# A third pair of k-tiles in the last half-pass of w_down, and five more loads

## The chip, the cores and the metric

The kernel runs on one core of one Trainium2 chip. The metric is the device time of one execution in microseconds (us). A core has engines with queues of their own, each in program order: TensorE (PE, with its weight loads as PEld), VectorE (DVE), ScalarE (ACT), GpSimd (POOL) and SyncE (SP), which here only issues DMAs. POOL issues DMAs too, among them those that add to what stands at the destination (accumulating DMAs). The kernel's order on every queue is the order in which the program text emits instructions; nothing is rescheduled afterwards.

## The reference

One layer of a hybrid block on 256 tokens of width 2048, in float32:

```python
xn = rms_norm(h, norm1_g[l])
proj = jnp.einsum('bsd,dn->bsn', xn, w_in[l])          # 2048 x 5120
...
h = h + jnp.einsum('bsm,md->bsd', mixed, w_out[l])     # mixed: attention and convolution, 2048 x 2048
hn = rms_norm(h, norm2_g[l])
a = jnp.einsum('bsd,df->bsf', hn, w_gate[l])           # 2048 x 5632
bu = jnp.einsum('bsd,df->bsf', hn, w_up[l])
h = h + jnp.einsum('bsf,fd->bsd', jax.nn.silu(a) * bu, w_down[l])   # 5632 x 2048
```

The change touches the last product, with w_down, and three loads elsewhere.

## The kernel before

**Precision.** Each float32 operand is split into hi (rounded to the matmul type, by ScalarE) and lo, the residue (operand minus hi, by VectorE). A product is three matmuls: hi with hi, lo with hi, hi with lo. A weight tile's residue is made in one of two ways: VectorE subtracts (L334), or ScalarE writes the negated copy (L328) and a POOL DMA adds the weights to it (L329). The second way takes work from VectorE and gives ScalarE and POOL some; a unit for which it is used has `by_dma` set.

**Units.** Weights are worked off in units (`chunks`), each with its load (SP), cast (ACT), residue and matmuls. Two kinds matter here:
- a "two" (`load_chunk`, `round_chunk`, `split_chunk`, `multiply_two`): two k-tiles of 128 rows, 512 columns of weights, for both halves m of the tokens: 2 x 2 x 3 = 12 matmuls. In w_down a "g" two belongs to the first 512 of a block of 1024 columns and a "u" two to the second; for the same two k-tiles both are needed.
- a "pair" ("s": `load_pair`, `round_pair`, `split_pair`, `multiply_pair`): two k-tiles k and k + 4, both column halves, both token halves as a 2 x 2 block product in Strassen's form with seven products instead of eight: 7 x 3 = 21 matmuls instead of 24. For that VectorE makes four sums of weight blocks (L1019 to L1021), ScalarE casts (L1022 the blocks, L1025 the sums) and VectorE makes residues (L1028 `wlb` of the blocks, L1029 `wlt` of the sums). The first product of a pair uses a sum, so its third matmul waits for `wlt`.

**w_down in passes.** The hidden dimension is done in groups of 4, 4 and 3 blocks of 512 (`FGROUPS`). After each group `down_pass` multiplies the group's k-tiles with w_down: two half-passes, i = 0 and 1, one for each 1024 columns of the output (n = 2 i). `NDS` says how many pairs a group's pass has; k-tiles 0 to 3 and 4 to 7 of a group can be paired, the others are twos. `DORDERS` writes out the order of the units of each half-pass. The last group (nb = 3, 12 k-tiles) has two pairs and four g and four u twos per half-pass; its second half-pass runs in the order g g g s g s u u u u.

**Forms of the activations.** `transposed` turns a block of silu(a) * up into k-tiles through the PE, two k-tiles (t = 0, 1) at a time. For tiles that are paired it keeps the raw copy (`raw_act`), for others hi and lo. When the second block of a group is through, `make_down_forms` makes the seven sums of activations and their residues, 11 VectorE and 7 ScalarE operations over nd k-tiles each, spread over the next block.

**Order and looking ahead** (`run_chunks`). Before the matmuls of unit t are emitted, units up to t + 2 have been cast and split; if a pair stands among units t to t + 3, casting (for a pair also L1019 to L1021) reaches to t + 3. Loads are emitted when the unit whose buffer they take has been split, or, if that unit's residue comes by DMA, not before its own matmuls' turn; plain weights have five buffers, pairs two. Casts have three buffers, so a cast waits for the PE to finish with the unit three before.

**What ends a half-pass.** After its last pair or g unit, `bank_sums` adds the eight PSUM banks up (L1156 to L1163); `down_half` and `down_whole` add the results into h, which lies in HBM (`hd`), by accumulating POOL DMAs (L1210, L1238). In the very last half-pass they are added in SBUF instead: `fetch_end` (L1200) loads h's last 1024 columns as `hend` when the first half-pass ends, L1212, L1217, L1278 and L1231 add, and the rows are stored. The first 1024 columns of the output are copied from `hd` (L1245).

**Other loads of the change.** `late_loads` (L185) loads the rope table ahead of unit 9; `x_whole` (L1298) loads x in token-major form ahead of unit 40. Both on SP's queue.

Of the kernel before, what the change touches and what calls it, by code (L numbers as in the profile page):

```python
# [18 lines left out]
P = 128  # L19
D = 2048  # L20
S = 256
NM = S // P
# [9 lines left out]
N = 512  # L32
# [52 lines left out]
ORDER = "sggsggsuusuu"  # L85
# [1 line left out]


HD = N // P
NDS = (4, 4, 2)  # L90
DORDERS = {4: (ORDER, ORDER), 3: ("gguusggsuu", "gggsgsuuuu")}
HD_LAG = 3
DOWN_BY_DMA = {4: (dict(g=(0, 1), u=(1,)),) * 2, 3: (dict(g=(), u=()),) * 2}

Q1, Q6, Q7, Q5, Q2, Q4, Q3, QX = range(8)

# [31 lines left out]
def tile_block(  # L128
# [6 lines left out]
    act, dve, pool, pe, sp = nc.scalar, nc.vector, nc.gpsimd, nc.tensor, nc.sync  # L135
# [13 lines left out]
    h = [pre.tile([P, D], F32, tag=f"h{m}", name=f"h{m}", bufs=1) for m in range(NM)]  # L149
    away = ctx.enter_context(tc.tile_pool(name="away", bufs=1, space=bass.MemoryType.DRAM))  # L150
    hd = [away.tile([P, D], F32, tag=f"hd{m}", name=f"hd{m}") for m in range(NM)]
# [25 lines left out]
    rt = pre.tile([P, NM, 2, DH], F32, tag="vb", name="rt")  # L177
# [3 lines left out]
    def late_loads():  # L181
        sp.dma_start(out=cw.rearrange("p c w -> p (c w)"), in_=conv_w)
        for t, v in ((gb, vecs[:2]), (lamv, vecs[2:])):
            sp.dma_start(out=t, in_=v.rearrange("(o v) d -> o v d", o=1).to_broadcast(list(t.shape)))
        sp.dma_start(out=rt, in_=rope.rearrange("(m p) c d -> p m c d", p=P))  # L185

    def late_constants():
        late_loads()
# [43 lines left out]
    def lhs_two(pfx, k):  # L232
        return tuple(lhs.tile([P, 2, S], F32R, tag=f"l{x}", name=f"{pfx}{x}{k}") for x in ("hi", "lo"))
# [12 lines left out]
    def start(gen):  # L246
        running.append(gen)
# [7 lines left out]
    def lag(n):  # L255
        for _ in range(n):
            yield
# [593 lines left out]
    def up_done(j, ps):  # L851
        fp = ffn["pool"]
        aa = []
        for m in range(NM):
            a = fp.tile([P, N], F32, tag=f"sum{2 + m}", name="a")
            dve.scalar_tensor_tensor(a, ps[m], rstd2[m], sil[m], ALU.mult, ALU.mult)
            aa.append(a)
        yield from lag(4)
        yield from transposed(j, aa)

    def transposed(j, aa):
        last = j + 1 in FIRSTS and NDS[group_of(j)[0]] < HD
        b = j - group_of(j)[1]
        for t in range(N // P // 2):

            pool_, tag = (acc_ps, "acc") if last else (aux_ps, "aux")
            pt = pool_.tile([P, 2, S], F32, tag=tag, name="ps_a")
            for i in range(2):
                for m in range(NM):
                    c = (2 * t + i) * P  # L870
                    pe.transpose(pt[:, i, m * P : (m + 1) * P], aa[m][:, c : c + P], ident)  # L871
            g = group_of(j)[0]
            nd = NDS[g]
            if b < 2 and 2 * t < nd:
                if not b and not t:
                    raw_act[g] = ffn["pool"].tile([P, 2, nd, S], F32, tag="draw", name="raw_act")
                act.copy(raw_act[g][:, b, 2 * t : 2 * t + 2, :], pt)
                yield from lag(3 if last else 6)
                if b and 2 * t + 2 == nd:
                    start(make_down_forms(g))  # L880
                continue
            hi, lo = lhs_two("a", j * (N // P) + 2 * t)
            act.copy(hi, pt)
            yield from lag(1 if last else 2)
            dve.tensor_tensor(lo, pt, hi.bitcast(F32), ALU.subtract)
            for i in range(2):
                actT[j * (N // P) + 2 * t + i] = (hi[:, i, :], lo[:, i, :])
            yield from lag(1 if last else 3 if closing(j) else 4)

    def closing(j):  # L890
        return j + 1 in FIRSTS and NDS[group_of(j)[0]] == HD

    def group_of(j):

        j0 = 0
        for g, nb in enumerate(FGROUPS):
            if j < j0 + nb:
                return g, j0
            j0 += nb

    raw_act = {}
    down_forms = {}

    def make_down_forms(g):

        nd = NDS[g]
        gap = lambda: lag(5 if FGROUPS[g] == 4 else 2)
# [195 lines left out]
    def fast_block(order, pairs, twos, sources, operands, half, whole, by_dma=dict(g=(), u=())):  # L1103

        units, sums = [], {}
        left = dict(s=list(pairs), g=list(twos), u=list(twos))
        for kind in order:
            what = left[kind].pop(0)
            c = dict(kind=kind, sums=sums, done=None, first={}, last={}, rows=what["rows"], **operands)
            if kind == "s":  # L1110
                c.update(p=what["p"], fetch=load_pair, by_dma=False, round=round_pair, split=split_pair, multiply=multiply_pair,
                         uses=[q for q, _, _ in PRODUCTS])
                c["from"] = sources
            else:
                w, col = sources[kind]
                c.update(ks=what["ks"], w=w, nk=2, width=N, cols=[(col, N)], by_dma=what["k"] in by_dma[kind],
                         load=load_chunk, round=round_chunk, split=split_chunk, multiply=multiply_two,
                         uses=(Q3, QX) if kind == "u" else (Q2, Q4))
            units.append(c)
        assert not any(left.values())  # L1120
        for q in range(8):
            users = [c for c in units if q in c["uses"]]
            users[0]["first"][q] = users[-1]["last"][q] = True
        [c for c in units if c["kind"] != "u"][-1]["done"] = half
        units[-1].update(done=whole, prompt=True)
        chunks.extend(units)
# [8 lines left out]

    def down_pass(g, j0, nb):
        k0 = j0 * HD
        nd = NDS[g]
        ks = [k for k in range(nb * HD) if k >= 2 * HD or k % HD >= nd]
        twos = [dict(ks=(k0 + a, k0 + b), rows=slice(k0 + a, k0 + b + 1, b - a), k=i)  # L1140
                for i, (a, b) in enumerate(zip(ks[::2], ks[1::2]))]
        for i, order in enumerate(DORDERS[nb]):
            n = 2 * i
            end = {}
            fast_block(order, [dict(p=p, rows=slice(k0 + p, k0 + p + HD + 1, HD)) for p in range(nd)], twos,
                       dict(g=(w_down, n * N), u=(w_down, (n + 1) * N)),
                       dict(pairs=lambda: down_forms.get(g), plain=actT.get),
                       lambda sums, n=n, end=end: down_half(g, n, sums, end),
                       lambda sums, n=n, end=end: down_whole(g, n, sums, end), DOWN_BY_DMA[nb][i])

# [23 lines left out]
    def block_done(j, q):  # L1174
        while "u" not in halfway:
            yield
        u = halfway.pop("u")
        for m, i in enumerate((Q3, QX)):
            dve.tensor_tensor(u[m], q[i], u[m], ALU.add)
        while "g" not in halfway:  # L1180
            yield
        g = halfway.pop("g")
        for m in range(NM):
            dve.tensor_tensor(u[m], u[m], g[m], ALU.mult)
        yield from lag(6 if closing(j) else 4)
        yield from transposed(j, u)


    hend = []
# [4 lines left out]
    def fetch_end():  # L1194

        t = ffn["pool"].tile([P, 7, NS, P], F32, tag="fhi", name="hend")
        t = t.rearrange("p a b c -> p (a b c)")
        for m in range(NM):
            hend.append(t[:, m * 2 * N : (m + 1) * 2 * N])
            sp.dma_start(out=hend[m], in_=hd[m][:, D - 2 * N :])  # L1200

    def down_half(g, n, q, end):
        gs, us = yield from bank_sums(q)
        if not at_end(g, n):
            end.update(us=us)
            yield from lag(HD_LAG)
        for m in range(NM):
            cs = slice(n * N, (n + 1) * N)
            if not at_end(g, n):
                pool.dma_start(out=hd[m][:, cs], in_=gs[m], accum_op=ALU.add)  # L1210
            else:
                dve.tensor_tensor(hend[m][:, :N], hend[m][:, :N], gs[m], ALU.add)  # L1212
                pool.dma_start(out=out[m * P : (m + 1) * P, cs], in_=hend[m][:, :N])
        yield
        if at_end(g, n):
            for m in range(NM):
                dve.tensor_tensor(hend[m][:, N:], hend[m][:, N:], us[m], ALU.add)  # L1217
        end.update(us=us)
# [76 lines left out]

    def x_whole():
        for m in range(NM):
            sp.dma_start(out=h[m], in_=x[m * P : (m + 1) * P, :])  # L1298

    for i in range(OPENING):  # L1300
        before[i] = opening(i)
# [31 lines left out]
```

## Time and profile before

| | |
|---|---|
| runs shown | 1036.13 us median of 3 (1036.13 to 1036.54) |
| the profiled execution | 1035.99 us, of which span 1034.2 us |
| granted TensorE clock | 1.000 |
| last w_down pass, second half: first matmul | 998.36 us after the span's start |
| HBM read and written | 204.24 MB and 9.44 MB |

How to read the lines: a timeline row has start, duration, engine, source line, operation, output tile <- input tiles, shape, count, and in brackets the engine's idle time before it with what ended it. Matmuls are pipelined, so their shown durations (0.39 us) overlap; the distance between starts is what one costs. A group row ends in total busy time and mean ns, then idle time before it. "q" after an engine's name marks its queue issuing a DMA. "DMA to landing" is the time from issue until the data is there.

### The profile page before, as it was taken

The numbers are of one execution on the slowest core, as the hardware profiler recorded it, in microseconds if no ns is written. First come the engines' busy times: TensorE is split into PE (matmuls) and PEld (weight loads), VectorE is DVE, ScalarE is ACT, GpSimd is POOL, SyncE is SP. The second block draws the span as 40 slices with busy tenths as digits, with TensorE's granted clock in tenths as the row PEclk, the third lists the DMA queues.
The fourth block names the chain that finished last, engine by engine and source line by source line (L and its number), as shares of the span: only waits on it lengthen the run. The fifth ranks groups of instructions, "written<-read, shape, count | busy, mean of one in ns | idle before, by whom it ended". The sixth has DMA issues, their size and how long they took to land.

```text
span 1034.2 us, 13010 instructions
## 1 busy us (share of the span) xinstructions
PE 1028.1 (99%) x4645; PEld 848.9 (82%) x4645; DVE 927.3 (90%) x1126; ACT 638.3 (62%) x780; POOL 108.7 (11%) x147
## 2 busy tenths in 40 slices
PE   9999999999999999999999999999999999999998
PEld 7888888888888888888888888888888888888886
DVE  7899999989766699999999898989999989989887
ACT  7554656655666575677666556667657556667452
POOL 0130112111000100100102111001001111000010
PEclk9999999999999999999999999999999999999999
DMA  9657654553546677987989899879798979797773
GB/s 340 225 182 276 215 175 145 183 183 135 183 171 223 189 258 226 286 256 211 260 260 257 265 255 271 267 225 261 230 270 248 280 214 298 231 262 230 218 219 106
DMA packets 115664, 237.59 MB, mean 230 GB/s; under 512 B 7696, under 2 KB 8848, under 8 KB 115344
## 3 DMA queue, kind: packets, MB, share of 16 engines
q1 hardware_dynamic: 104720, 203.58, 59.0%
q0 software_dynamic: 10592, 33.04, 16.5%
q8 instruction: 36, 0.59, 0.2%
q14 instruction: 28, 0.23, 0.1%
q10 hardware_dynamic: 288, 0.16, 0.1%
HBM read 204.24 MB, written 9.44 MB: 207 GB/s over the span
## 4 chain that ended last, share of the span: by engine, by line
PE 96%; DVE 2%; DMA 1%; issue 1%; ACT 0%; SPq 0%; DVEq 0%
PE acc L364 11%; PE acc L365 11%; PE acc L370 11%; PE q L1067 11%; PE q L1068 11%; PE q L1073 11%; PE q L1048 9%; PE q L1046 9%; PE q L1047 9%; PE ps_a L871 1%; DVE wlo L334 1%; DMA raw<-in_w_in_dram 1%; PE ps_s L692 1%; PE ps_o L762 1%; DVE wlt L1029 0%
## 5 line engine op out<-in xcount | busy, mean ns | idle before, releaser
L325 ACT CAST whi<-raw 128x1024 fp32r<-128x1024 f32 (+1 forms) x257 | 266.4, 1047 | 149.7 <-PE acc L365 87.5
L334 DVE TENSOR_TENSOR wlo<-raw,whi 128x1024 fp32r<-128x1024 f32 (+1 forms) x211 | 254.6, 1217 | 37.9 <-ACT whi L325 37.8
L1025 ACT CAST wh<-wt 128x2048 fp32r<-128x2048 f32 x60 | 114.9, 1915 | 108.8 <-DVE wt L1021 108.7
L1029 DVE TENSOR_TENSOR wlt<-wt,wh 128x2048 fp32r<-128x2048 f32 x60 | 137.4, 2290 | 19.5 <-ACT wh L1025 19.4
L364 PE MATMUL acc<-whi,xhi 128*128 128x512 f32 x320 | 127.2, 398 | 0.7 <-ACT whi L325 0.6
L1067 PE MATMUL q<-whi,chi 128*128 128x512 f32 x320 | 125.2, 391 | 0.0
L365 PE MATMUL acc<-whi,xlo 128*128 128x512 f32 x320 | 125.1, 391 | 0.0
L1068 PE MATMUL q<-whi,clo 128*128 128x512 f32 x320 | 124.6, 389 | 0.0
L1046 PE MATMUL q<-wh,fhi 128*128 128x512 f32 x280 | 109.9, 392 | 0.0
L1047 PE MATMUL q<-wh,flo 128*128 128x512 f32 x280 | 108.9, 389 | 0.0
L1028 DVE TENSOR_TENSOR wlb<-wb,wh 128x1536 fp32r<-128x1536 f32 x60 | 105.1, 1751 | 1.1 <-ACT wh L1022 1.1
L553 DVE SCALAR_TENSOR_TENSOR y<-upad,cw,y 128x256 f32<-128x256 f32 x240 | 102.2, 485 | 2.2 <-ACT y L546 2.2
L329 POOL DMA_DIRECT2D wlo<-raw x46 | 39.8, 865 | 508.0 <-ACT wlo L328 283.4
L1022 ACT CAST wh<-wb 128x1536 fp32r<-128x1536 f32 x60 | 88.3, 1472 | 0.0
L370 PE MATMUL acc<-wlo,xhi 128*128 128x512 f32 x320 | 87.1, 393 | 0.0
L1073 PE MATMUL q<-wlo,chi 128*128 128x512 f32 x320 | 85.6, 389 | 0.0
L1067 PE MATMUL q<-whi,ahi 128*128 128x512 f32 x190 | 74.1, 390 | 0.0
L1068 PE MATMUL q<-whi,alo 128*128 128x512 f32 x190 | 74.0, 389 | 0.0
L1019 DVE TENSOR_TENSOR wt<-wb 128x1024 f32<-128x1024 f32 x60 | 73.1, 1218 | 0.0
L364 PEld LDWEIGHTS acc<-whi,xhi 128*128 128x128 f32 x320 | 60.3, 189 | 14.5 <-ACT whi L325 2.0
L365 PEld LDWEIGHTS acc<-whi,xlo 128*128 128x128 f32 x320 | 60.3, 188 | 12.3
L1073 PEld LDWEIGHTS q<-wlo,chi 128*128 128x128 f32 x320 | 60.1, 188 | 12.6
(253 smaller groups left out, 1836.3 us busy)
## 6 DMA issues: line engine op xcount, KB each, us to landing
raw<-in_w_in_dram SPq DMA_DIRECT2D x79, 512.0 KB, 4.7
raw<-in_w_gate_dram SPq DMA_DIRECT2D x48, 512.0 KB, 5.3
raw<-in_w_up_dram SPq DMA_DIRECT2D x48, 512.0 KB, 5.3
raw<-in_w_down_dram SPq DMA_DIRECT2D x48, 512.0 KB, 6.4
wlo<-raw POOLq DMA_DIRECT2D x46, 512.0 KB, 7.1
wb<-in_w_up_dram SPq DMA_DIRECT2D x40, 512.0 KB, 4.5
wb<-in_w_gate_dram SPq DMA_DIRECT2D x40, 512.0 KB, 5.8
wb<-in_w_down_dram SPq DMA_DIRECT2D x40, 512.0 KB, 6.0
```

The source lines that it names most:

```text
L325: act.copy(c["hi"], c["raw"])
L334: dve.tensor_tensor(c["lo"], c["raw"], c["hi"].bitcast(F32), ALU.subtract)
L364: pe.matmul(ps[m], xhi[:, ms], hi[:, j, :], start=c["first"] and j == 0, stop=False)
L365: pe.matmul(ps[m], xlo[:, ms], hi[:, j, :], start=False, stop=False)
L370: pe.matmul(ps[m], xhi[:, ms], lo[:, j, :], start=False, stop=c["last"] and j == nk - 1)
L1025: act.copy(c["hi"][:, :SUMMED], c["t"])
L1029: dve.tensor_tensor(lot, c["t"], c["hi"][:, :SUMMED].bitcast(F32), ALU.subtract)
L1046: pe.matmul(ps, hi, c["hi"][:, w], start=bool(first), stop=False)
L1047: pe.matmul(ps, lo, c["hi"][:, w], start=False, stop=False)
L1067: pe.matmul(ps, xs[i][0][:, ms], hi[:, i, :], start=i == 0 and bool(c["first"].get(qs[m])), stop=False)
L1068: pe.matmul(ps, xs[i][1][:, ms], hi[:, i, :], start=False, stop=False)
L1073: pe.matmul(sum_bank(c, qs[m]), xs[i][0][:, ms], lo[:, i, :], start=False, stop=i == 1 and bool(c["last"].get(qs[m])))
```

## The change

The second half-pass of the last group gets three pairs instead of two (`PASS_PAIRS`, the first half-pass keeps two): its twos fall from four g and four u to three and three, and the order becomes g s g s g s u u u. The first two g twos of that half-pass get their residues by accumulating DMA, those of the first half-pass stay with VectorE. The activations' forms of that group are made over three k-tiles instead of two; k-tiles 2 and 6 of the group are kept both raw and as hi and lo, since the first half-pass still uses them as plain tiles. The rope table is loaded in two transfers instead of one, x in four instead of two, and h's end in four instead of two; bytes are the same.

```diff
@@ -87,10 +87,11 @@
 
 
 HD = N // P
-NDS = (4, 4, 2)
-DORDERS = {4: (ORDER, ORDER), 3: ("gguusggsuu", "gggsgsuuuu")}
+NDS = (4, 4, 3)
+PASS_PAIRS = ((4, 4), (4, 4), (2, 3))
+DORDERS = {4: (ORDER, ORDER), 3: ("gguusggsuu", "gsgsgsuuu")}
 HD_LAG = 3
-DOWN_BY_DMA = {4: (dict(g=(0, 1), u=(1,)),) * 2, 3: (dict(g=(), u=()),) * 2}
+DOWN_BY_DMA = {4: (dict(g=(0, 1), u=(1,)),) * 2, 3: (dict(g=(), u=()), dict(g=(0, 1), u=()))}
 
 Q1, Q6, Q7, Q5, Q2, Q4, Q3, QX = range(8)
 
@@ -182,7 +183,8 @@
         sp.dma_start(out=cw.rearrange("p c w -> p (c w)"), in_=conv_w)
         for t, v in ((gb, vecs[:2]), (lamv, vecs[2:])):
             sp.dma_start(out=t, in_=v.rearrange("(o v) d -> o v d", o=1).to_broadcast(list(t.shape)))
-        sp.dma_start(out=rt, in_=rope.rearrange("(m p) c d -> p m c d", p=P))
+        for m in range(NM):
+            sp.dma_start(out=rt[:, m], in_=rope[m * P : (m + 1) * P])
 
     def late_constants():
         late_loads()
@@ -874,11 +876,14 @@
             if b < 2 and 2 * t < nd:
                 if not b and not t:
                     raw_act[g] = ffn["pool"].tile([P, 2, nd, S], F32, tag="draw", name="raw_act")
-                act.copy(raw_act[g][:, b, 2 * t : 2 * t + 2, :], pt)
-                yield from lag(3 if last else 6)
-                if b and 2 * t + 2 == nd:
+                end = min(2 * t + 2, nd)
+                act.copy(raw_act[g][:, b, 2 * t : end, :], pt[:, : end - 2 * t])
+                if 2 * t + 2 <= PASS_PAIRS[g][0]:
+                    yield from lag(3 if last else 6)
+                if b and end == nd:
                     start(make_down_forms(g))
-                continue
+                if 2 * t + 2 <= PASS_PAIRS[g][0]:
+                    continue
             hi, lo = lhs_two("a", j * (N // P) + 2 * t)
             act.copy(hi, pt)
             yield from lag(1 if last else 2)
@@ -1135,11 +1140,11 @@
 
     def down_pass(g, j0, nb):
         k0 = j0 * HD
-        nd = NDS[g]
-        ks = [k for k in range(nb * HD) if k >= 2 * HD or k % HD >= nd]
-        twos = [dict(ks=(k0 + a, k0 + b), rows=slice(k0 + a, k0 + b + 1, b - a), k=i)
-                for i, (a, b) in enumerate(zip(ks[::2], ks[1::2]))]
         for i, order in enumerate(DORDERS[nb]):
+            nd = PASS_PAIRS[g][i]
+            ks = [k for k in range(nb * HD) if k >= 2 * HD or k % HD >= nd]
+            twos = [dict(ks=(k0 + a, k0 + b), rows=slice(k0 + a, k0 + b + 1, b - a), k=i)
+                    for i, (a, b) in enumerate(zip(ks[::2], ks[1::2]))]
             n = 2 * i
             end = {}
             fast_block(order, [dict(p=p, rows=slice(k0 + p, k0 + p + HD + 1, HD)) for p in range(nd)], twos,
@@ -1197,7 +1202,9 @@
         t = t.rearrange("p a b c -> p (a b c)")
         for m in range(NM):
             hend.append(t[:, m * 2 * N : (m + 1) * 2 * N])
-            sp.dma_start(out=hend[m], in_=hd[m][:, D - 2 * N :])
+        for a in range(0, 2 * N, N):
+            for m in range(NM):
+                sp.dma_start(out=hend[m][:, a : a + N], in_=hd[m][:, D - 2 * N + a : D - N + a])
 
     def down_half(g, n, q, end):
         gs, us = yield from bank_sums(q)
@@ -1295,7 +1302,8 @@
 
     def x_whole():
         for m in range(NM):
-            sp.dma_start(out=h[m], in_=x[m * P : (m + 1) * P, :])
+            for a in range(0, D, D // 2):
+                sp.dma_start(out=h[m][:, a : a + D // 2], in_=x[m * P : (m + 1) * P, a : a + D // 2])
 
     for i in range(OPENING):
         before[i] = opening(i)
```

## The prediction

> **What bounds the kernel now.** The page came first: how full TensorE is and what the chain of waits is made of.
>
> ```profile
> span 1034.2 us, 13010 instructions
> PE 1028.1 (99%) x4645; PEld 848.9 (82%) x4645; DVE 927.3 (90%) x1126; ACT 638.3 (62%) x780; POOL 108.7 (11%) x147
> PE 96%; DVE 2%; DMA 1%; issue 1%; ACT 0%; SPq 0%; DVEq 0%
> ```
>
> TensorE is busy from end to end, VectorE nearly so. A PE-bound kernel is shortened by fewer matmuls and by gaps that close. So the next views are the waits and PE's timeline in the stage that the edit rebuilds, the second half of the last w_down pass (from 998.36 us).
>
> ```profile
> 998.36 0.39 PE L1067 MATMUL q<-whi,ahi 128*128 128x512 f32 x1
> 1001.08 0.39 PE L1067 MATMUL q<-whi,ahi 128*128 128x512 f32 x1
> ...
> 1014.19 0.39 PE L1046 MATMUL q<-wh,dhs 128*128 128x512 f32 x1
> 1014.42 0.39 PE L1047 MATMUL q<-wh,dls 128*128 128x512 f32 x1
> 1015.03 0.50 PE L1048 MATMUL q<-wlt,dhs 128*128 128x512 f32 x1 [0.23 <-DVE wlt L1029]
> ...
> 1019.47 0.39 PE L1067 MATMUL q<-whi,ahi 128*128 128x512 f32 x1
> ```
>
> The first two rows start neighbouring twos, twelve matmuls apart: 2.72/12 = 0.2267 us each (the 0.39 is a pipelined duration), so a pair of 21 needs 4.76. From 1001.08 to 1014.19 stand three twos and the first pair, 12.92 us of matmuls in 13.11: 0.19 lost. From 1014.19 to 1019.47 stands the second pair: 5.28 for 4.76, 0.52 lost, and the row with the wait shows where (0.61 instead of 0.23 before its third matmul). **The stage holds 0.71 us of stall**, PE waiting for `wlt`, the last thing VectorE makes of a pair.
>
> ```profile
> 987.32 3.49 DVE L334 TENSOR_TENSOR wlo<-raw,whi 128x1024 fp32r<-128x1024 f32 x3
> 992.38 0.69 DVE L1158 TENSOR_TENSOR sum<-q,sum 128x512 f32<-128x512 f32 x1 [1.57 <-ACT sum L1156]
> 996.37 1.22 DVE L334 TENSOR_TENSOR wlo<-raw,whi 128x1024 fp32r<-128x1024 f32 x1
> 998.11 1.29 DVE L1226 TENSOR_TENSOR sum<-q,sum 128x512 f32<-128x512 f32 x2 [0.52 <-PE q L1073]
> 999.31 1.21 DVE L1019 TENSOR_TENSOR wt<-wb 128x1024 f32<-128x1024 f32 x1
> 1003.03 1.75 DVE L1028 TENSOR_TENSOR wlb<-wb,wh 128x1536 fp32r<-128x1536 f32 x1
> 1004.70 2.28 DVE L1029 TENSOR_TENSOR wlt<-wt,wh 128x2048 fp32r<-128x2048 f32 x1
> 1006.90 1.22 DVE L334 TENSOR_TENSOR wlo<-raw,whi 128x1024 fp32r<-128x1024 f32 x1
> 1008.03 1.22 DVE L1019 TENSOR_TENSOR wt<-wb 128x1024 f32<-128x1024 f32 x1
> 1010.62 1.75 DVE L1028 TENSOR_TENSOR wlb<-wb,wh 128x1536 fp32r<-128x1536 f32 x1
> 1012.69 2.29 DVE L1029 TENSOR_TENSOR wlt<-wt,wh 128x2048 fp32r<-128x2048 f32 x1 [0.31 <-ACT wh L1025]
> 1014.90 3.49 DVE L334 TENSOR_TENSOR wlo<-raw,whi 128x1024 fp32r<-128x1024 f32 x3
> 1018.93 0.69 DVE L1158 TENSOR_TENSOR sum<-q,sum 128x512 f32<-128x512 f32 x1 [0.55 <-ACT sum L1156]
> ```
>
> Costs on VectorE, as distances between starts: a residue 1.13; L1019 to L1021 2.59 (1008.03 to 1010.62); L1028 1.67; L1029 2.20; the six bank sums 3.99 (992.38 to 996.37); the two of L1226 1.20. A pair whose ScalarE cast comes after L1021 takes 6.87 from L1019 to whatever follows L1029 (1008.03 to 1014.90). From 987 to 1015 VectorE idles little; it decides when each pair may run.
>
> **The matmuls.** Ten units become nine: eight twos of 12 matmuls and two pairs of 21 (138) become six and three (135). Three fewer, 3 x 0.2267 = **-0.68 us**. The order strings fix these counts, so that the change removes less than this is no case.
>
> **VectorE's order, walked through.** New order g s g s g s u u u; the first two g residues come by DMA. The looking ahead puts the first pair's L1019 to L1021 behind the residues of the last two units of the first half: 987.32 + 2 x 1.13 = 989.6, to 992.2, hidden in the 1.57 us wait that the second row shows. The sums keep 992.38 to 996.37. Then the first pair's L1028 and L1029 to 1000.24, L1226 to 1001.44 (2.1 later than now), the second pair to 1008.31, the one g residue still made here to 1009.44, the third pair's L1029 done 6.95 after that (1008.03 to 1012.69 + 2.29 now), 1016.39.
> PE wants them at: first pair from 1001.08, third matmul 1001.53; second pair from 1001.08 + 4.76 + 2.72 = 1008.56, so 1009.01; third from 1016.04, so 1016.49. The margins are 1.3, 0.6 and 0.05 us (now a wlt is used 0.05 after it is done). So the stalls close, **-0.71 us**; bounds 0 (they merely move) and -0.71, and I take the full figure since the walk ends without a stall, by almost nothing. What L1226 now delays: the bank it frees is first written by the first pair's last product, 1001.08 + 18 x 0.2267 = 1005.2, no wait.
>
> **The tail.** PE ends at 998.36 + 6 x 2.72 + 3 x 4.76 = 1028.96 (now 998.36 + 8 x 2.72 + 2 x 4.76 + 0.71 = 1030.35). Sums of the last half start when the third pair's fifth product is out: now 18.93 - 14.19 less 0.52 of stall = 4.22 after its start, so 1020.26, behind the u residues, which end at 1019.8. Then 3.99 and four additions at 0.6: 1026.7, where L1278 may go at 1026.5 and the final L1231 at 1027.8: 0.5 us of room after L1278's own 0.6. Nothing; a VectorE later by 1 us would cost 0.4.
>
> **Residues by DMA.**
>
> ```profile
> 987.50 1.05 ACT L325 CAST whi<-raw 128x1024 fp32r<-128x1024 f32 x1 [0.52 <-ACT whi L325]
> 994.93 1.05 ACT L325 CAST whi<-raw 128x1024 fp32r<-128x1024 f32 x1 [2.58 <-PE q L1068]
> L329 POOL DMA_DIRECT2D wlo<-raw x46: 852/862/943, 407.4 to 954.9; - x46
> DMA to landing us min/median/max: 5.4/7.1/9.6
> ```
>
> Each adds a second ScalarE pass of the cast's size, 1.05 us, and one transfer on POOL. First: cast at 987.5 as now, negated copy to 989.6, landed 996.7 to 999.2; wanted at 998.36 + 8 x 0.2267 = 1000.2. Second: its cast waits for a buffer as 994.93 does, copy to 997.0, landed 1004.2 to 1006.7; wanted at 1005.84 + 1.81 = 1007.65. Both hidden, the second by 1 us at worst. Behind the second on POOL stand the additions to h (L1210 1.5 us later, L1238 2); landing 11.8 us (below) after 1003 at worst, they leave their reader, the copy to the output, some 18 us. Behind the first's landing SP holds the load of the last u unit: it can be issued at some 1001, and its weights are cast at 1016.
>
> **The third pair's weights** take the buffer of the first pair, free after its L1028 at 998.04. SP then issues two loads, the four of h's end and the last u unit's.
>
> ```profile
> L1009 SPq DMA_DIRECT2D wb<-in_w_down_dram x2: 368/415/462, 984.8 to 985.2; - x2
> DMA to landing us min/median/max: 3.9/4.4/4.9
> ...
> L1200 SPq DMA_DIRECT2D hend<-hd x2: 423/476/528, 998.1 to 998.7; - x2
> DMA to landing us min/median/max: 9.8/10.8/11.8
> q1 hardware_dynamic: 104720, 203.58, 59.0%
> q0 software_dynamic: 10592, 33.04, 16.5%
> ```
>
> Bounds: 4.9 us where POOL sends nothing, 11.8 where it adds to h. By position on SP's queue (second of 512 KB, as hend's first now) I take 9.8: 998.5 + 9.8 = 1008.3, ahead of the 1009.44 at which VectorE wants it. Hidden, with 1.1 us of room.
> The Trainium skill, DMA: Bandwidth & Descriptors, section Queues, rings and completion order, says that each engine takes turns between the queue rows that have work, so POOL's adding transfers would slow these loads. The trace agrees (4.4 against 10.8 us). By that rule the sum loses its room, which is the first rival.
>
> **Larger forms, and the other loads.**
>
> ```profile
> L932 DVE TENSOR_TENSOR dlo<-raw_act,dhi 128x256 fp32r<-128x256 f32 x2 | 0.8, 420 | 0.0
> 951.14 2.29 DVE L1029 TENSOR_TENSOR wlt<-wt,wh 128x2048 fp32r<-128x2048 f32 x1 [0.28 <-ACT wh L1025]
> 955.90 0.39 PE L1046 MATMUL q<-wh,fhi 128*128 128x512 f32 x1
> 960.13 0.69 DVE L1158 TENSOR_TENSOR sum<-q,sum 128x512 f32<-128x512 f32 x1 [2.23 <-ACT sum L1156]
> ACT whi L325 <- DMA raw<-in_w_in_dram: 0.6, 2, 0.3
> ```
>
> Eleven VectorE operations grow from 256 elements (0.42) halfway to 512 (0.69), 0.13 each, 1.45 us. Five stand before the L1029 of 951.14, which ends at 953.43, 2.9 us before the pair of 955.90 needs it at its third matmul; the rest falls into the 2.23 us wait. Two more ScalarE copies, under 1.05 each (a cast of four times the size), lie in the 38% that it idles. Uncovered it would be 1.45.
> Five more transfers are five times some 0.48 us of SP's issuing (the L1200 row above), the same bytes. Casts waited for loads only twice up to 130 us, 0.3 each, and PE not for those. Zero; at most 2.4 us if SP's issuing bounded a stage.
>
> **Sum.** 1035.99 (this execution: 1034.2 span and 1.8 around it) - 0.68 - 0.71 = 1034.60. The median of the runs lies 0.14 above that execution: **1034.7 us**.
>
> **Rivals.**
> (1) The third pair's weights come late. It decides from 1009.44; from 1010.9 the 1.39 us are gone and the kernel is slower than before. q0 takes 0.165 x 1034.2 / 33.04 = 5.2 us of all engines per MB, so the new 0.5 MB of residue ahead of them may add 2.6 us: to the 1008.3, 1010.9, which is 1.5 late, 1036.2; to the worst landing (11.8), 998.5 + 11.8 + 2.6 = 1012.9, 3.5 late, **1038.2**. For it: margin 0.05 behind, so every microsecond reaches PE. Against: these loads stand first on SP's queue, and L1238's additions now come later than they do.
> (2) VectorE stays behind and the pairs wait as now, only elsewhere: only the matmuls count, **1035.45**. For it: three pairs in a row of 30 us instead of two, and 0.05 us of margin. Against: two residues gone and an idle 1.57 us used.
> (3) More than forecast: **1033.9** would need another 0.8 us, and neither PE's 10 us of other irregular steps nor the 3.6 us after its last matmul is touched.
>
> **How the numbers follow.** Forecast 0.60 (1034.3 to 1035.1), (2) 0.16, (1) 0.20, half of it at its upper price, (3) 0.04. A measurement of this kernel can tell about 0.2%, 2.07 us, from no change. Under 1034.06 lies (3): 0.04. Over 1038.20 lies the upper half of (1) and a little for a stall not seen here: 0.13. Between: 0.83. Range 1034.2 to 1037.0: left out are 0.04 below and some 0.15 above.
>
> **What would show it.** Right: 4642 matmuls; no PE wait for `wlt` over 0.2 us after 998; first pair's L1019 near 989.6; both residues landed before 1000 and 1007; the third pair's L1019 starting without an idle time put down to a load; last matmul near 1029. Wrong: VectorE idle before that L1019 with a DMA as releaser, a PE wait for `wlo` from a DMA, or stalls before 960 us.

## The result and the profile after

The changed kernel takes 1034.73 us (median of 19 runs, 1034.16 to 1035.33) against 1036.67 us (19 runs, 1035.86 to 1037.18) for the kernel before on the same chips: a ratio of 0.9983, 95% interval 0.9976 to 0.9989, so 0.7 to 2.5 us faster. The page after, and PE's timeline in the rebuilt half-pass (line numbers have moved, in the lines shown by two to seven: L1048 is now L1053, L1029 is L1034, L1009 is L1014):

```profile
span 1032.5 us, 13023 instructions
PE 1027.2 (99%) x4642; PEld 849.1 (82%) x4642; DVE 930.6 (90%) x1127; ACT 642.7 (62%) x784; POOL 110.5 (11%) x149
```

```profile
998.25 0.39 PE L1072 MATMUL q<-whi,ahi 128*128 128x512 f32 x1
...
1015.93 0.39 PE L1051 MATMUL q<-wh,dhs 128*128 128x512 f32 x1
1016.16 0.39 PE L1052 MATMUL q<-wh,dls 128*128 128x512 f32 x1
1016.39 0.44 PE L1053 MATMUL q<-wlt,dhs 128*128 128x512 f32 x1
1016.66 0.39 PE L1051 MATMUL q<-wh,dls 128*128 128x512 f32 x1
...
1028.75 0.40 PE L1095 MATMUL qe<-wlo,ahi 128*128 128x256 f32 x2
```

Three matmuls fewer, as counted. The third pair begins 17.68 us after the half-pass does, which is what three twos and two pairs need (3 x 2.72 + 2 x 4.76); the step behind its third matmul is 0.27 us instead of 0.23, and that 0.04 is all that is left of the stalls. From the half-pass's first matmul to the start of the last one it is 30.61 us, before 31.95. VectorE's timeline after, the same stretch as in the prediction:

```profile
987.21 2.35 DVE L336 TENSOR_TENSOR wlo<-raw,whi 128x1024 fp32r<-128x1024 f32 x2
989.48 1.22 DVE L1024 TENSOR_TENSOR wt<-wb 128x1024 f32<-128x1024 f32 x1
...
992.27 0.69 DVE L1163 TENSOR_TENSOR sum<-q,sum 128x512 f32<-128x512 f32 x1
...
997.93 2.29 DVE L1034 TENSOR_TENSOR wlt<-wt,wh 128x2048 fp32r<-128x2048 f32 x1
1000.14 1.28 DVE L1233 TENSOR_TENSOR sum<-q,sum 128x512 f32<-128x512 f32 x2
1001.34 1.21 DVE L1024 TENSOR_TENSOR wt<-wb 128x1024 f32<-128x1024 f32 x1
...
1009.33 1.22 DVE L1024 TENSOR_TENSOR wt<-wb 128x1024 f32<-128x1024 f32 x1
...
1013.98 2.29 DVE L1034 TENSOR_TENSOR wlt<-wt,wh 128x2048 fp32r<-128x2048 f32 x1 [0.32 <-ACT wh L1030]
1016.19 3.49 DVE L336 TENSOR_TENSOR wlo<-raw,whi 128x1024 fp32r<-128x1024 f32 x3
1020.21 0.69 DVE L1163 TENSOR_TENSOR sum<-q,sum 128x512 f32<-128x512 f32 x1 [0.54 <-ACT sum L1161]
```

Every row stands within 0.15 us of the walk in the prediction (the half-pass itself begins 0.11 us earlier than there). The long wait for the sums (1.57 us before) is filled by the first pair's L1024, and between 987 and 1020 nothing on VectorE waits for a load. Of SP's and POOL's transfers in that stretch, issue to landing:

```profile
L331 POOL DMA_DIRECT2D wlo<-raw x2: 859/870/882, 989.9 to 997.2; - x2
...
DMA to landing us min/median/max: 6.0/7.1/8.1
...
L1014 SPq DMA_DIRECT2D wb<-in_w_down_dram x2: 367/437/507, 998.1 to 998.5; - x2
...
DMA to landing us min/median/max: 6.7/7.9/9.1
...
L1207 SPq DMA_DIRECT2D hend<-hd x4: 583/656/1234, 999.1 to 1001.8; - x4
...
DMA to landing us min/median/max: 10.7/11.9/13.2
```

The two residues landed at 998.0 and 1003.3, the third pair's weights at 1007.6, 1.8 us before VectorE reached for them (1009.33). One load came closer than the prediction had it: the last u unit's, issued at 1002.5, landed 13.8 us later, at 1016.3. ScalarE waited 0.5 us for it, PE did not.

What the trace holds that the forecast did not is at the very end. The next section takes it apart; the table has, for every kernel run, the length of the rebuilt half-pass (first matmul to the start of the last) and the time from the last store's landing to the end of the span, both read from the traces.

```
kernel                                      half-pass   landing to end   median us (runs)
before                                          31.95             1.23   1036.67 (19)
changed                                         30.61             0.91   1034.73 (19)
e0 changed, again                               30.61             0.91   1034.78 (11)
e1 third pair, no split loads                   30.63             1.22   1035.10 (11)
e2 before, five split loads                     31.99             0.92   1036.14 (11)
e3 changed, all residues by VectorE             32.67             0.92   1036.64 (11)
e4 before, two residues by DMA                  31.95             1.22   1036.74 (11)
e5 changed, one VectorE operation more          31.89             0.91   1035.96 (11)
e6 changed, third pair's weights late           38.75             0.92   1042.70  (5)
e7 third pair, five more loads, all of x        30.64             0.92   1034.59 (11)
e8 third pair, two more loads                   30.64             1.10   1034.80 (11)
```

The medians come from four sets of runs on different chips; the kernel before had 1036.67 us in the first, 1036.62 beside e0 to e3, 1036.23 beside e4 to e6 and 1036.45 beside e7 and e8. The two columns repeat to 0.04 us where the program in that stretch is the same, while whole runs scatter by some 1 us. Most of that scatter which the profiles show is at the start: the half-pass begins anywhere from 998.25 to 999.06 us, and some 200 matmuls in, at 47.84 to 48.58 us, the kernels are already that far apart. So differences of a few tenths are read from the columns, not from the medians.

### The profile page after: what moved, and what is told of

Its sections match the earlier page's. It is cut to its first block, busy times and chain, and to the rows that moved or that the text cites. A ratio compares the mean times of both kernels' runs of the same rounds, so it can differ in the third digit from the quotient of the medians.

```text
span 1032.5 us, 13023 instructions
## 1 busy us (share of the span) xinstructions
PE 1027.2 (99%) x4642; PEld 849.1 (82%) x4642; DVE 930.6 (90%) x1127; ACT 642.7 (62%) x784; POOL 110.5 (11%) x149
## 4 chain that ended last, share of the span: by engine, by line
PE 98%; DVE 1%; DMA 1%; issue 0%; SPq 0%; ACT 0%; DVEq 0%
PE acc L366 11%; PE acc L367 11%; PE q L1072 11%; PE acc L372 11%; PE q L1078 11%; PE q L1073 11%; PE q L1053 9%; PE q L1051 9%; PE q L1052 9%; PE ps_a L873 1%; DMA raw<-in_w_in_dram 1%; PE ps_s L694 1%; PE ps_o L764 1%; DVE wlo L336 0%; PE ps_h L815 0%; PE ps_qk L675 0%
## 5 line engine op out<-in xcount | busy, mean ns | idle before, releaser
L336 DVE TENSOR_TENSOR wlo<-raw,whi 128x1024 fp32r<-128x1024 f32 (+1 forms) x207 | 249.4, 1216 | 36.9 <-ACT whi L327 36.6
L1034 DVE TENSOR_TENSOR wlt<-wt,wh 128x2048 fp32r<-128x2048 f32 x61 | 139.7, 2291 | 19.7 <-ACT wh L1030 19.6
L1024 DVE TENSOR_TENSOR wt<-wb 128x1024 f32<-128x1024 f32 x61 | 74.3, 1219 | 0.0
L366 PEld LDWEIGHTS acc<-whi,xhi 128*128 128x128 f32 x320 | 60.4, 189 | 14.2 <-ACT whi L327 1.7
L1072 PE MATMUL q<-whi,ahi 128*128 128x512 f32 x182 | 71.1, 391 | 0.0
L1073 PE MATMUL q<-whi,alo 128*128 128x512 f32 x182 | 70.9, 390 | 0.0
```

What stands on the lines that cost most here:

```text
L336: dve.tensor_tensor(c["lo"], c["raw"], c["hi"].bitcast(F32), ALU.subtract)
L366: pe.matmul(ps[m], xhi[:, ms], hi[:, j, :], start=c["first"] and j == 0, stop=False)
L1034: dve.tensor_tensor(lot, c["t"], c["hi"][:, :SUMMED].bitcast(F32), ALU.subtract)
L1072: pe.matmul(ps, xs[i][0][:, ms], hi[:, i, :], start=i == 0 and bool(c["first"].get(qs[m])), stop=False)
L1073: pe.matmul(ps, xs[i][1][:, ms], hi[:, i, :], start=False, stop=False)
```

## The experiments

**e0, the changed kernel again**, as yardstick.

> The changed kernel again, as the yardstick for the next three on the same chip. Theory (VectorE's order sets when a pair may run; the gain is three matmuls, 0.68 us, and 0.71 us of closed stalls; the transfers are worth nothing): 1.4 us under the kernel before, ratio 0.9987. Rival (the five transfers or something outside the last half-pass give the other 0.5 us of the measured 1.9): 1.9 us, ratio 0.9982.

Ratio 0.9983 (0.9974 to 0.9991), half-pass and end as in the first profile. 1.84 us under the kernel before in the same session: nearer to the rival's 1.9 than to 1.4, with an interval that holds both.

**e1, the third pair without the split loads**, and **e2, the split loads without the third pair.** In e1 the three loads are as before, in e2 they are the only edit:

```diff
-        for m in range(NM):
-            sp.dma_start(out=rt[:, m], in_=rope[m * P : (m + 1) * P])
+        sp.dma_start(out=rt, in_=rope.rearrange("(m p) c d -> p m c d", p=P))
...
-        for a in range(0, 2 * N, N):
-            for m in range(NM):
-                sp.dma_start(out=hend[m][:, a : a + N], in_=hd[m][:, D - 2 * N + a : D - N + a])
+            sp.dma_start(out=hend[m], in_=hd[m][:, D - 2 * N :])
...
-            for a in range(0, D, D // 2):
-                sp.dma_start(out=h[m][:, a : a + D // 2], in_=x[m * P : (m + 1) * P, a : a + D // 2])
+            sp.dma_start(out=h[m], in_=x[m * P : (m + 1) * P, :])
```

> The third pair and its residues by DMA, but rope table, x and h's end loaded in as few transfers as before. Theory: the same as the changed kernel within 0.2 us, third pair and its waits at the same places. Rival: 0.5 us slower than the changed kernel, as the split transfers would carry that part.

> The kernel before with the five more transfers alone. Theory: the same as before within 0.2 us (ratio 1.000), both waits for wlt in the last half-pass still there. Rival: 0.5 us faster than before (ratio 0.9995).

Ratios 0.9985 (0.9976 to 0.9994) and 0.9997 (0.9988 to 1.0006). Medians: e1 0.32 us behind e0, e2 0.48 ahead of the kernel before, both towards the rival, neither decisive alone. The table decides: the half-pass belongs to the third pair (30.63 against 31.99), the end belongs to the loads (1.22 against 0.92). So the split loads are worth 0.31 us after all, and not where they are issued. At the end SP waits for eight DMA semaphores, one after the other in a fixed order. The transfers that SP and ScalarE issue take these eight strictly in turn, 395 of them in the kernel before and 400 in the changed one; POOL's 78 and 80 have eight others. When SP was past each of these waits, by the trace, in us:

```
before:  ... 1032.04 (1st)  1032.54 (2nd)  1033.01 (3rd: last store)  1033.07 (4th)  1033.13  1033.19  1033.25  1033.31 (8th)
changed: ... 1030.12 (5th)  1030.63 (6th)  1031.15 (7th)  1031.65 (8th: last store)
```

Before, the last store's semaphore is the third (395 is 49 times eight and three); five further waits of 0.06 us come after it though nothing is left to land. Five more transfers move the last store on by five places, to the eighth.

**e7 and e8** test that against the place of the loads. e7 leaves rope table and h's end whole and loads x in seven transfers, e8 splits x alone, as the change does:

```diff
...
         for m in range(NM):
+            cuts = (0, 512, 1024, 1536, D) if m else (0, 512, 1024, D)
+            for a, b in zip(cuts, cuts[1:]):
+                sp.dma_start(out=h[m][:, a:b], in_=x[m * P : (m + 1) * P, a:b])
```

> Found in the runs so far: after the last store has landed, the kernels with the five more transfers need 0.92 us to the end and those without 1.23, because SP at the end waits for eight DMA semaphores one after the other (0.06 us each), and with five more transfers the last store has the last of the eight instead of the third. This kernel has the third pair, the rope table and h's end in as few transfers as before, and x in seven instead of two: five more, but all at 93 us. Theory (only the count modulo eight matters): 0.92 us after the last landing, the last store on the last semaphore, time as the changed kernel, ratio near 0.9982. Rival (the place of the split loads matters, h's end above all): 1.23 us, as with the pairs alone, 0.3 us slower than the changed kernel.

> The third pair with x alone split as in the change: two more transfers. Theory (count modulo eight): the last store's semaphore is two further on than without, three waits follow it: 3 x 0.06 = 0.18 us more than with five, so 1.10 us from the last landing to the end. Rival (place): 0.92 or 1.23.

0.92 and 1.10 us, to the hundredth, with the last store on the eighth and on the fifth semaphore. Ratios 0.9983 (0.9974 to 0.9992) and 0.9981 (0.9972 to 0.9989), which could not have told the two apart. The place of the loads does not count; their number does, and as the semaphores are taken in turn, it counts modulo eight (no kernel was run with eight more). POOL's transfers do not enter: e3 has two fewer than the changed kernel and e4 two more than the one before, and the last store keeps its semaphore.

**e3, the residues of the last half-pass all by VectorE:**

```diff
-DOWN_BY_DMA = {4: (...) * 2, 3: (dict(g=(), u=()), dict(g=(0, 1), u=()))}
+DOWN_BY_DMA = {4: (...) * 2, 3: (dict(g=(), u=()),) * 2}
```

> The changed kernel with the residues of the last half-pass all made by VectorE, none by DMA. Theory: the first one moves the sums from 992.3 to 993.2, the second stands ahead of the second pair, so VectorE is 2.1 us later at the second and third pair; their margins are 0.6 and 0.05, so PE waits some 1.4 us at the second and 0.6 more at the third, 2.0 us in all: ratio to before about 1.0005. Rival (VectorE has room, the residues by DMA do little): ratio as the changed kernel, 0.9985. The landing of the third pair's second load tells what the residue in the queues ahead of it costs: by the estimate of 5.2 us per MB, up to 2.6 us earlier than the 9.1 us after issue that the changed kernel shows.

Ratio 0.9999 (0.9990 to 1.0008), half-pass 32.67, 2.06 us longer than the changed kernel's. PE's rows with a wait in e3:

```profile
1010.76 0.50 PE L1053 MATMUL q<-wlt,dhs 128*128 128x512 f32 x1 [1.31 <-DVE wlt L1034]
1018.76 0.50 PE L1053 MATMUL q<-wlt,dhs 128*128 128x512 f32 x1 [0.23 <-DVE wlt L1034]
```

The steps before these two are 1.70 and 0.61 us, each followed by one of 0.34: 1.58 and 0.49 lost. The third pair alone, without the residues by DMA, gives back more than it saves: the half-pass is 0.72 us longer than the one before, and the whole time is level with it only because the end is 0.31 shorter and the medians scatter. One part of the expectation missed: without a residue in the queues the third pair's second load landed 11.0 us after issue, not earlier than 9.1 but later. It is issued 1.3 us later here. Why it took longer, and what a residue costs the other transfers, is not shown by this pair of runs.

**e4, the residues by DMA alone**, in the kernel before:

```diff
-DOWN_BY_DMA = {4: (...) * 2, 3: (dict(g=(), u=()),) * 2}
+DOWN_BY_DMA = {4: (...) * 2, 3: (dict(g=(), u=()), dict(g=(0, 1), u=()))}
```

> The kernel before (two pairs, order g g g s g s u u u u) with the residues of the first two g units of the last half-pass by DMA and nothing else. Theory: of the two residues taken from VectorE only the second counts, since the first lies in front of a wait of 1.57 us; VectorE is 1.13 us earlier at both pairs, so the 0.71 us of waits for wlt close; but the second residue is wanted at 1002.9 here and lands near 1003.3, so up to 0.5 us of a new wait. In all 0.2 to 0.7 us faster than before (ratio 0.9993 to 0.9998). Rival (the stalls are not VectorE's doing): the waits for wlt stay, ratio 1.000.

No gain: ratio 1.0004 (0.9995 to 1.0012), half-pass 31.95 as before. The waits of PE's weight loads between 998 and 1018 (total us, times, longest):

```profile
PEld q L1073 <- DMA wlo<-raw: 0.6, 1, 0.6
PEld q L1048 <- DVE wlt L1029: 0.4, 1, 0.4
```

And the two residues, issue to landing:

```profile
L329 POOL DMA_DIRECT2D wlo<-raw x2: 859/868/877, 990.7 to 998.0; - x2
...
DMA to landing us min/median/max: 5.6/8.0/10.4
```

The waits for `wlt` shrink (the steps around them lose 0.25 us instead of 0.67) and a wait for a residue takes their place (0.42): the same sum. It is not the residue that I had named. The second landed in 5.6 us; the first needed 10.4, because the loads behind it in the program now had to wait for their units' turn, and SP, with nothing else to issue, sent h's end (1 MB) already at 990.8, beside it. That h's end is what slowed it is not tested by itself, but in the seven other kernels that make this residue by DMA, h's end goes out from 998.8 on, when the residue has landed, and the residue takes 7.7 to 8.1 us. In the changed kernel the third pair's load, which waits for VectorE until 998.1, keeps h's end behind it, and the first residue lands in 8.1. The median is 0.51 us above the kernel before of the same set; of that, e4's profile shows 0.35 lost in the first half-pass, where PE waits for another residue at 965.7, which no other profile has. Whether this belongs to the edit is open.

**e5, one VectorE operation more:** the first subtraction of the second pair done twice; the second writes the same values over the first.

```diff
-        dve.tensor_tensor(t[:, 2:4], b[:, 1:3], ..., ALU.subtract)
+        for _ in range(1 + (c is [u for u in chunks if u.get("kind") == "s"][-2])):
+            dve.tensor_tensor(t[:, 2:4], b[:, 1:3], ..., ALU.subtract)
```

> The changed kernel with VectorE's first subtraction of the second pair done twice: 1.25 us more on VectorE, nothing else, same numbers out. Theory: the margins are 0.6 us at the second pair and 0.05 at the third, so PE waits 0.6 us at the second and 1.2 us by the third in all: 1.2 to 1.4 us slower than the changed kernel, ratio to before 0.9995 to 1.0000. Rival (only PE bounds the half-pass): no change, ratio 0.9985.

Half-pass 31.89, 1.28 us longer than the changed kernel's: an operation of 1.25 us on VectorE comes out at the end whole. The ratio to before is 0.9995 (0.9986 to 1.0004), so 0.27 us faster where e0 was 1.84; by the medians the operation costs 1.6 us, with the scatter of both in it. Its PE waits:

```profile
1010.39 0.50 PE L1054 MATMUL q<-wlt,dhs 128*128 128x512 f32 x1 [0.51 <-DVE wlt L1035]
1018.38 0.50 PE L1054 MATMUL q<-wlt,dhs 128*128 128x512 f32 x1 [0.22 <-DVE wlt L1035]
```

The steps around these waits lose 0.79 and 0.49 us, for 0.6 and 0.6 expected. That PE is 99% busy says nothing against it: with the third pair's margin used up, VectorE's order bounds this stretch.

**e6, the third pair's weights late:** `fetch_end()` is called between the pair's two loads instead of at the end of the first half-pass.

```diff
             sp.dma_start(out=c["b"][:, 2 * i : 2 * i + 2, :], in_=...)
+            if not i and c is [u for u in chunks if u.get("kind") == "s"][-1]:
+                fetch_end()
```

> The changed kernel with the four loads of h's end put between the two loads of the third pair's weights on SP's queue: the same transfers in another order. Theory: the pair's second load then lands where h's end landed last, near 1015, 5.6 us after VectorE could begin (1009.3), and as the margin behind is 0.05 us, the kernel is 5 to 6 us slower than the changed one, with VectorE idle before the third pair's first subtraction and a load as releaser. Rival (loads run side by side, order on the queue matters little): the second load lands by 1010 and under 1 us is lost.

The second load landed 14.2 us after its issue, at 1016.1, behind h's end as the theory had it (1.1 us later than its 1015); the loss is larger than it said, 8.1 us in the half-pass and 1042.70 us in all, ratio 1.0062 (1.0048 to 1.0076). The second load on the one hand, VectorE's timeline and PE's on the other, in e6:

```profile
L1014 SPq DMA_DIRECT2D wb<-in_w_down_dram x2: 367/467/567, 998.3 to 1001.9; - x2
...
DMA to landing us min/median/max: 8.0/11.1/14.2
```

```profile
1016.20 1.23 DVE L1026 TENSOR_TENSOR wt<-wb 128x1024 f32<-128x1024 f32 x1 [6.56 <-issue]
...
1020.86 0.79 PE L1053 MATMUL q<-wh,dhs 128*128 128x512 f32 x1 [4.54 <-ACT wh L1032]
1021.45 0.63 PE L1054 MATMUL q<-wh,dls 128*128 128x512 f32 x1
1023.19 0.79 PE L1055 MATMUL q<-wlt,dhs 128*128 128x512 f32 x1 [1.11 <-DVE wlt L1036]
...
1024.20 0.63 PE L1054 MATMUL q<-wh,dls 128*128 128x512 f32 x1
1024.63 0.63 PE L1055 MATMUL q<-wlt,dls 128*128 128x512 f32 x1
```

And three windows of it: length, then busy time and count of PE, PEld, DVE, ACT and POOL, the granted TensorE clock, DMA share, GB/s.

```profile
1005.00:1015.00 10.00, 10.00 (x45) 8.28 (x45) 4.33 (x3) 2.12 (x2) 0.58 (x1) 1.00 1.08 275
1015.00:1021.00 6.00, 1.47 (x7) 0.89 (x5) 4.44 (x5) 3.56 (x3) 0.53 (x1) 0.88 0.93 222
1021.00:1026.00 5.00, 3.89 (x9) 2.59 (x10) 5.00 (x4) 2.65 (x3) 0.00 (x0) 0.50 0.01 4
```

VectorE's row names "issue" for its 6.56 us of idling, no load; but it starts 0.1 us after the second load's landing. The half-pass begins at 998.48 here, 0.23 later than in the changed kernel. Counted from there, VectorE starts the pair 6.64 us later than in the changed kernel (1016.20 against 1009.33), and the pair's third matmul is 6.57 late (1023.19 against 1016.39). The other 1.6 us come after it: following 4.5 us without a matmul the clock is granted at 0.50, and matmuls step by 0.43 us instead of 0.23 until 1026. The Trainium skill, TensorE: Matmul & The Clock Gate, section What's actually happening, says that an idle window of about 3.4 us halves the array's clock and that a busy one gives it back. The trace agrees: 4.5 us of idling, and 0.50 for the window after it.

## Why the prediction was right, and where a step was off

- **Three matmuls, -0.68, and the stalls, -0.71:** the half-pass is 1.34 us shorter, for a forecast 1.39. The missing 0.05 is lost at the third pair, in the step of 0.27 us and the ones behind it: the margin of 0.05 us that the walk had left was just used up. e3 and e5 show that nothing more was to spare: 2.06 and 1.28 us are lost for 2.1 and 1.25 put on VectorE. e3 and e4 also show that neither half of the change gives the gain alone: the pair without the residues by DMA lengthens the half-pass by 0.72, the residues without the pair leave it at 31.95.
- **The taken values** held: the third pair's second load took 9.1 us for 9.8 taken (bounds 4.9 and 11.8), the residues 8.1 and 6.0 for 7.1 to 9.6. The last u unit's load (13.8 us) went beyond the 11.8 that the prediction calls the worst, without harm. The reckoning of 5.2 us of all engines per MB that priced the first rival is not borne out by any run.
- **The larger forms** cost what the step said (0.55 us per operation of 384 elements for 0.42) and stayed hidden: before 960 us PE's weight loads wait for the same things as in the kernel before, none of them longer, and at 953.5 us PE stands within 0.15 us of where it stood.
- **The five transfers at zero was wrong, by 0.31 us.** The step counted SP's issue time and asked only which stage could be slowed; the bounds, 0 and +2.4, did not go below nothing. The third rival went wrong with it, where it said that the time after the last matmul is untouched: 0.31 us of that time are five waits that a different number of transfers removes. The traces thus show 1.34 + 0.31 = 1.65 us, and the spans 1.7. That the forecast of 1034.7 was met to 0.03 us is also luck: it took 1.4 us off a median of three runs that lies 0.54 us below that of the 19, and the measured change is 1.94. The two errors, a base too low and a gain too small, cancel.
- **The remaining 0.2 to 0.3 us** between the medians' 1.84 to 1.94 us and the traces' 1.65 is within the interval; no run shows a cause.
- **The rivals:** (1) the late weights did not occur, but e6 shows its mechanism: of 6.64 us that VectorE starts later, 6.57 reach PE, and after 4.5 us of idling the clock added 1.6. (2), VectorE staying behind, is what e3 is, and it costs more than the rival's price: not the stalls of before but 2.06 us. None of the versions run beats the changed kernel in the traces: e7's half-pass and end are the same as its.

## What to carry to other kernels

Saving matmuls with a form that costs more VectorE work pays only if that work is found a place: walk the in-order queue through and compare when each operand is done with when PE wants it; a margin of 0.05 us was enough, and one operation too many cost its full length. Whether taking work off an engine helps depends on where it stands: a residue in front of a wait is free to begin with. And a program that takes turns among a fixed number of semaphores ends sooner or later by which of them its last store holds, so a change in the number of loads or stores anywhere can move the end by some tenths of a microsecond.

## What the runs showed of the hardware that was not expected

- After the last store lands, SP's remaining waits cost 0.06 us each even though their semaphores had long been reached: 0.31 us for five, 0.18 for three (1.23, 1.10 and 0.92 us from landing to end).
- After 4.5 us without a matmul the granted clock was 0.50 for about 5 us, in a kernel that had 1.00 up to 1015; that added 1.6 us to a delay of 6.57 (e6).
- Two residues of 0.5 MB by DMA landed in 10.4 and 5.6 us within one half-pass (e4), the slower with h's end issued beside it; no run tests h's end as the cause by itself.
